# Rotating images by 180 degrees on one Trainium2 core: the first 2 KB of the last 32 rows loaded, brought in by three small transfers

## The chip, the cores and the metric

The kernel runs on one core of one Trainium2 chip. The metric is the device time of one execution in microseconds (us); less is better. The time of an execution is a little longer than its span, which runs from the first to the last instruction of the program in the profile.

## The reference

```python
x = np.random.randn(32, 3, 256, 256).astype(np.float32)

def reference(x):
    return np.rot90(x, k=2, axes=(-2, -1)).astype(np.float32)
```

Each of the 96 images of 256 x 256 float32 numbers is turned by 180 degrees. Seen as one row of 65,536 numbers, an image is simply reversed. Nothing is computed: 25.17 MB are read from HBM, put into reverse order within each image, and 25.17 MB are written.

## The kernel before

**Tiling.** An image is cut into four quarters of E = 16,384 numbers (64 KB). A tile has 128 partitions of E numbers, so it holds 32 images, one quarter in each partition; the whole input is three such tiles, `A`, `Bt` and `Ct`, which all stay in SBUF beside a scratch tile `T`. What follows calls one partition's 64 KB a row. Partition 4n + s holds quarter s of image n.

**Reversal.** It has two halves. VectorE (DVE) reverses every row in place: `swap` copies a piece from the row's end, read backwards, to `T`; then the mirror piece from the row's beginning, backwards, to the end; then `T` to the beginning. `turn` does this for a whole tile, in 4 pieces of 2048 columns for `A` and `Ct` (12 copies), and in 6 pieces of up to 1366 columns for `Bt` (18 copies). The store transfers do the rest: they write the four quarters of an image in reverse order (`o4[g][:, ::-1, lo:hi]`).

**Order of the transfers.** All transfers are issued by SP (SyncE) on one DMA queue, which feeds 16 DMA engines. The loads are issued at the very beginning, without any wait: `A` (line 56), `Bt` (line 56), then `Ct` in three parts (line 72): the 64 even rows, the 32 rows 1, 5, 9, ..., called `ahead`, and the 32 rows 3, 7, 11, .... In the trace's packet records each row is one packet, and between the small packets that tell of a transfer's end each DMA engine has 8 rows of `A`, 8 of `Bt`, then 4, 2 and 2 rows of `Ct`; then 8 rows of each of the three stores.

**When the first store is issued.** Tile dependencies would let the store of `A` go once `A` is turned. Two dependencies written by hand hold it back:

```python
*_, last_but_one, last = turn(Bt, 6)
after(last_but_one, ahead,
      "this copy starts when all loads but two rows are in")
first = store(A, 0, 0, E)
after(first, last, "the first store goes two copies after that")
```

The last but one copy of `Bt`'s turn waits until `ahead` has landed; after it comes the last copy, and then SP issues the stores of `A` and `Bt` (line 59). The turn of `Ct` waits for all three parts of `Ct`, and the store of `Ct` comes after that.

Of the kernel before, what the change touches and what calls it, by code (L numbers as in the profile page):

```python
# [2 lines left out]

os.environ.setdefault("NEURON_RT_ULTRASERVER_MODE", "4")

# [4 lines left out]


@with_exitstack
def kernel(
    ctx: ExitStack,
    tc: tile.TileContext,
    x: bass.AP,
    out: bass.AP,
):
    nc = tc.nc  # L20
    P = 128

    B, C, H, W = x.shape
    L = H * W
    G = 32
    E = L // 4
    J = E // 8

    x4 = x.rearrange("b c h w -> (b c) (h w)").rearrange(
        "(g n) (s e) -> g (n s) e", n=G, s=4)  # L30
    o4 = out.rearrange("b c h w -> (b c) (h w)").rearrange(
        "(g n) (s e) -> g n s e", n=G, s=4)

    pool = ctx.enter_context(tc.tile_pool(name="slots", bufs=1))
    A = pool.tile([P, E], x.dtype, tag="A")
    Bt = pool.tile([P, E], x.dtype, tag="B")
    Ct = pool.tile([P, E], x.dtype, tag="C")
    T = pool.tile([P, J], x.dtype, tag="T")

    def back(t, lo, hi):  # L40
        return t[:, hi - 1:(lo - 1 if lo else None):-1]

    def copy(dst, src):
        c = nc.vector.tensor_copy(out=dst, in_=src)  # L44
        tc.keep_in_program_order(c)
        return c

    def after(later, earlier, why):
        tc.add_manual_dep(
            later.ins, earlier.ins.name,  # L50
            mybir.DependencyInfo(
                mybir.DependencyClass.Sync, mybir.DependencyReason.DATA),
            reason=why)

    def load(t, g, lo, hi):
        return nc.sync.dma_start(out=t[:, lo:hi], in_=x4[g][:, lo:hi])  # L56

    def store(t, g, lo, hi):
        return nc.sync.dma_start(
            out=o4[g][:, ::-1, lo:hi], in_=t[:, lo:hi])  # L60

    def swap(t, lo, w):
        hi = E - lo - w
        return [
            copy(T[:, 0:w], back(t, hi, hi + w)),
            copy(t[:, hi:hi + w], back(t, lo, lo + w)),
            copy(t[:, lo:lo + w], T[:, 0:w])]

    half = E // 2

    def rows(first, step):
        return nc.sync.dma_start(
            out=Ct[first::step, :], in_=x4[2][first::step, :])

    load(A, 0, 0, E)
    load(Bt, 1, 0, E)
    rows(0, 2)
    ahead = rows(1, 4)
    rows(3, 4)

    def turn(t, pieces):
        done = []
        step = -(-half // pieces)
        for lo in range(0, half, step):
            done += swap(t, lo, min(step, half - lo))
        return done

    turn(A, 4)
# [5 lines that stand above are left out]
    store(Bt, 1, 0, E)  # L94
    turn(Ct, 4)
    store(Ct, 2, 0, E)


# [1 line left out]
_INS = ['x']  # L100
_OUTS = [((32, 3, 256, 256), 'float32')]


# [23 lines left out]
```

## Time and profile before

| | before |
|---|---|
| median of 3 runs | 122.09 us (121.94 to 122.11) |
| the profiled execution: time, span | 122.06 us, 120.3 us |
| DMA queue: share of 16 engines, mean rate | 97.3%, 418 GB/s |
| DVE busy | 45.2 us (38%), 42 copies |
| landing of `A` after its issue | 22.0 us |
| landing of the store of `Ct` after its issue | 42.7 us |

The profile counts the packets of the DMA engines, the copies on DVE and the issuing instructions of SP. A wait is put down to what ended it. In a view of the DMA, a packet's bytes are counted in the slice in which the packet starts, so that a high rate in a short slice says that several rows start there, and the number of rows can be read from it: a row of 64 KB in a slice of 0.2 us shows as 328 GB/s.

### The profile page before, as it was taken

The page shows a single profiled execution, that of the slowest core. Times are in us where ns is not written, and L with a number is a line of the kernel's source. Part 1 is how long each engine was busy: PE and PEld are TensorE (multiplying, and loading weights), DVE is VectorE, ACT ScalarE, POOL GpSimd, SP SyncE. Part 2 cuts the span into 40 slices and gives each one's busy share as a digit, 9 for nine tenths or more (in the row PEclk, how much of TensorE's full clock was granted, in tenths as well). Part 3 has the DMA queues.
Part 4 walks back from the last instruction along what each step waited for, and adds up shares of the span by engine and source line. Part 5 has one row for each costly group of instructions (what it writes and reads, how often), then busy time and mean ns, then how long its engine had stood idle before and what let it go on. Part 6 is the DMA issues. An engine that isn't in the chain of part 4 may idle for free.

```text
span 120.3 us, 101 instructions
## 1 busy us (share of the span) xinstructions
DVE 45.2 (38%) x42; POOL 0.2 (0%) x4
## 2 busy tenths in 40 slices
DVE  0000000499995099999459999400000000000000
POOL 0000000000000000000000000000000000000000
DMA  9889998899889988998899889988998889888980
GB/s 349 349 349 392 588 414 349 371 610 414 349 349 610 436 349 349 567 479 349 349 501 545 349 349 414 632 349 349 392 654 349 349 349 697 349 349 349 676 371 0
DMA packets 897, 50.33 MB, mean 418 GB/s; under 512 B 129, under 2 KB 129, under 8 KB 129
## 3 DMA queue, kind: packets, MB, share of 16 engines
q1 hardware_dynamic: 896, 50.33, 97.3%
q14 instruction: 1, 0.00, 0.0%
HBM read 25.17 MB, written 25.17 MB: 418 GB/s over the span
## 4 chain that ended last, share of the span: by engine, by line
DMA 34%; DVE 26%; another core or an unknown queue 2%; issue 1%; SPq 0%; DVEq 0%
DMA Bt<-in_x_dram 34%; DVE Bt L44 9%; DVE T L44 9%; DVE Ct L44 8%; SPq L56 0%; DVEq L44 0%
## 5 line engine op out<-in xcount | busy, mean ns | idle before, releaser
L44 DVE COPY T<-A 128x2048 f32<-128x2048 f32 x4 | 4.9, 1227 | 22.9 <-DMA A<-in_x_dram 22.8
L44 DVE COPY T<-Bt 128x1366 f32<-128x1366 f32 (+1 forms) x6 | 5.2, 874 | 4.5 <-DMA Bt<-in_x_dram 4.3
L44 DVE COPY T<-Ct 128x2048 f32<-128x2048 f32 x4 | 4.9, 1227 | 3.2 <-DMA Ct<-in_x_dram 3.1
L44 DVE COPY Bt<-T 128x1366 f32<-128x1366 f32 (+1 forms) x6 | 5.2, 872 | 0.2
L44 DVE COPY Bt<-Bt 128x1366 f32<-128x1366 f32 (+1 forms) x6 | 5.2, 872 | 0.2
L44 DVE COPY Ct<-T 128x2048 f32<-128x2048 f32 x4 | 4.9, 1227 | 0.1
L44 DVE COPY A<-A 128x2048 f32<-128x2048 f32 x4 | 4.9, 1227 | 0.1
L44 DVE COPY A<-T 128x2048 f32<-128x2048 f32 x4 | 4.9, 1227 | 0.1
L44 DVE COPY Ct<-Ct 128x2048 f32<-128x2048 f32 x4 | 4.9, 1227 | 0.1
L111 POOL MEMSET const-bfloat16-1.0<- 128x1 bf16 x1 | 0.1, 101 | 0.0
L111 POOL MEMSET const-uint8-127<- 128x1 uint8 x1 | 0.1, 101 | 0.0
L111 POOL MEMSET const-float32-0.0<- 128x1 f32 x1 | 0.1, 98 | 0.2 <-issue 0.2
L111 POOL MEMSET const-float32-1.0<- 128x1 f32 x1 | 0.1, 98 | 0.0
## 6 DMA issues: line engine op xcount, KB each, us to landing
Ct<-in_x_dram SPq DMA_DIRECT2D x3, 54.4
A<-in_x_dram SPq DMA_DIRECT2D x1, 22.0
Bt<-in_x_dram SPq DMA_DIRECT2D x1, 40.9
out_dram<-A SPq DMA_DIRECT2D x1, 22.3
out_dram<-Bt SPq DMA_DIRECT2D x1, 40.9
out_dram<-Ct SPq DMA_DIRECT2D x1, 42.7
```

The source lines that it names most:

```text
L44: c = nc.vector.tensor_copy(out=dst, in_=src)
L111: nc = _bacc.Bacc("TRN2", target_bir_lowering=False, num_devices=1)
```

## The change

The last of the loads, rows 3, 7, 11, ..., 127 of `Ct`, loses its first W = 512 columns (2 KB of each row). These 32 pieces are brought by three transfers of their own, of 15, 10 and 7 rows, which are issued after the even rows and before `ahead`. `ahead` itself, the copies and the stores stay as they are.

```diff
-    def rows(first, step):
+    def rows(first, step, end=P, lo=0, hi=E):
         return nc.sync.dma_start(
-            out=Ct[first::step, :], in_=x4[2][first::step, :])
+            out=Ct[first:end:step, lo:hi], in_=x4[2][first:end:step, lo:hi])
 
     load(A, 0, 0, E)
     load(Bt, 1, 0, E)
     rows(0, 2)
+    first, W = 3, 512
+    for k in (15, 10, 7):
+        rows(first, 4, first + 4 * (k - 1) + 1, 0, W)
+        first += 4 * k
     ahead = rows(1, 4)
-    rows(3, 4)
+    rows(3, 4, lo=W)
```

In the built program SP has three more transfers (15x512, 10x512, 7x512), and the last load is 32x15872 in place of 32x16384. The copies on DVE are the same 42 in the same order. The first copy of `Ct`'s turn waits for the even rows and the last load, and the second one, which reads the beginnings of the rows, for the three small transfers.

## The prediction

> **What bounds the kernel now.** I read the page's slices and its DMA queue first, then the waits, then the order of time where loads hand over to stores, then the DMA in short stretches. The page:
>
> ```profile
> DMA  9889998899889988998899889988998889888980
> GB/s 349 349 349 392 588 414 349 371 610 414 349 349 610 436 349 349 567 479 349 349 501 545 349 349 414 632 349 349 392 654 349 349 349 697 349 349 349 676 371 0
> q1 hardware_dynamic: 896, 50.33, 97.3%
> ```
>
> The 16 DMA engines are busy from the first slice to the last; the uneven rates are only whole rows counted where they start. In the packet records a 64 KB row takes 2.42 us on its engine, load or store (27.1 GB/s), and each engine has 24 rows to load and 24 to store: 48 x 2.42 = 116.2 us of a span of 120.28. So time can come or go only at the edges: the start, the handover from loads to stores, and the differences between the engines. DVE waits for transfers:
>
> ```profile
> DVE T L44 <- DMA A<-in_x_dram: 22.8, 1, 22.8
> DVE T L44 <- DMA Bt<-in_x_dram: 4.3, 1, 4.3
> DVE T L44 <- DMA Ct<-in_x_dram: 3.1, 1, 3.1
> ```
>
> There is one wait for each tile; `last_but_one`, which waits for `ahead`, is not among them. The order of time at the handover:
>
> ```profile
> 55.82 0.87 DVE L44 COPY T<-Bt 128x1362 f32<-128x1362 f32 x1
> 56.73 0.87 DVE L44 COPY Bt<-Bt 128x1362 f32<-128x1362 f32 x1
> 57.63 0.87 DVE L44 COPY Bt<-T 128x1362 f32<-128x1362 f32 x1
> 58.53 0.62 SPq L59 DMA_DIRECT2D out_dram<-A  x1
> 59.19 0.60 SPq L59 DMA_DIRECT2D out_dram<-Bt  x1
> 61.59 1.23 DVE L44 COPY T<-Ct 128x2048 f32<-128x2048 f32 x1 [3.09 <-DMA Ct<-in_x_dram]
> ```
>
> The copy at 56.73 follows the one at 55.82 at the usual step of 0.91 us: `ahead` had just landed. In the semaphore records its last of 16 landings is at 56.63, a slack of 0.10 us. The store goes at 58.53. How far the engines are apart is seen in short stretches, first where `ahead` ends and the last rows begin:
>
> ```profile
> 55.40:55.60 0.20, 0.20 (x1) 0.00 (x0) 1.00 1.52 655
> 55.60:55.80 0.20, 0.19 (x1) 0.00 (x0) 1.00 3.79 1638
> 55.80:56.00 0.20, 0.18 (x1) 0.00 (x0) 1.00 3.79 1638
> 56.00:56.20 0.20, 0.20 (x1) 0.00 (x0) 1.00 2.28 983
> 56.20:56.40 0.20, 0.20 (x1) 0.00 (x0) 1.00 0.76 328
> ```
>
> The last column is GB/s; 328 in 0.2 us is one row. So 2, 5, 5, 3 and 1 engines begin their last two rows in these stretches: the first engine is some 0.76 us ahead of the last (packets at 55.46 to 56.23), and as all rows take the same time, this lag is as old as the first row. Then the stores, from 60.2 to 61.4 in slices of 0.03 us:
>
> ```profile
> DMA  0000000099009099000099900099900000000000
> GB/s 0 0 0 0 0 0 0 0 2185 2185 0 0 2185 0 4369 4369 0 0 0 0 2185 6554 4369 0 0 0 2185 2185 2185 0 0 0 0 0 0 0 0 0 0 0
> ```
>
> 2185 is one row that starts there. Thirteen engines start storing from 60.45 to 60.87, three at 61.00, 61.03 and 61.06. The packet records of the loads end at 60.32 to 61.06. Sorted against the starts, the last three, and four more, go over to the stores within 0.01 us: their own loads are the limit. The other nine stand idle for some 0.1 us each (0.91 us in sum): the store's issue is their limit, the latest at 60.87. From there an engine needs 57.95 to 58.16 us for its 24 rows of stores, and the last ends at 119.13 (it began at 61.03). The last landing is at 119.47, and 0.81 us of closing make the span.
>
> **The change, part by part.** Sums are made against the profiled execution, 122.06 us (span 120.28, and 1.78 around it); the median of the runs, 122.09, is 0.03 above.
>
> *Three more issues on SP.* The three part transfers of `Ct` took 0.577, 0.586 and 0.597 us to issue. Three more move the issue of `ahead` from 2.24 to about 4.1 us and of the last load from 2.87 to about 4.8. The engines come to `ahead` at 50.6 us, so 46 us of earlier rows hide it: nothing. Without that cover it would be 3 x 0.63 = 1.9 us.
>
> *Bytes.* They are the same in sum. A piece of 2 KB is 1/32 of a row: 2.42 / 32 = 0.076 us. Each engine's last two rows lose 2 x 0.076 = 0.15 us. The transfers of 128, 64 and 32 rows gave each engine the same number of whole rows; going by them, 15, 10 and 7 rows are one row on each of 15, 10 and 7 engines. If all three begin at the same engine, seven engines have 3 pieces, three have 2, five have 1, and one has none: net +0.08, 0, -0.08 and -0.15 us. If they were spread evenly the net is 0. No row of this trace shows which engines they are. [...]
>
> *The price of a piece beyond its bytes.* From below: at every border between two transfers the packet records show the little end packet (9 ns) and the next row 6 ns after its start, and that row takes the usual 2.418 us. From above: the very first rows, with nothing in front of them, took 2.86 to 3.65 us, so 0.44 to 1.23 us of start that nothing hid. The pieces stand in a full queue behind a 64 KB row, as the borders do, so I take 0.01 us and keep 0.44 for the range. [...]
>
> *The wait for `ahead`.* The pieces go ahead of it, so an engine with three reaches its end 3 x 0.086 = 0.26 us later, one with two 0.17, with one 0.09. The slack is 0.10. What counts is the latest engine, at 56.22 by its end packet and 56.63 by its landing. If it is among the seven with three pieces, `ahead` lands at 56.89 and `last_but_one` starts 0.16 us late; with two, 0.07; with one or none, on time. Behind that copy stand the last copy, SP's issue of both stores, and the nine engines that are idle at the handover.
>
> *The handover.* With 0.16 us the latest of those nine starts storing at 61.03 and ends at 61.03 + 58.16 = 119.19. The late engines that have three pieces end their loads 0.08 + 3 x 0.01 = 0.11 us later: 61.14 to 61.17, and 58.0 to 58.1 us of stores make 119.15 to 119.24. Against 119.13 that is 0.06 to 0.11 us more. The turn of `Ct` begins at most 0.2 us later; it ends at 76.70, and its store is not reached by an engine before 99, so that costs nothing.
>
> Forecast: 122.06 + 0.1, rounded with the median's 0.03 to **122.2 us**, which is no change within the 0.2% (0.24 us) that a measurement of this kernel can tell.
>
> **The rivals.**
>
> *Evened out (faster side).* The late engines are those with one piece or none. Then `ahead` lands on time, the three late ones gain 0.08 to 0.15 us, and the end is set by the nine that wait for the store: 60.87 + 58.16 = 119.03, a gain of 0.10 us: 122.0. More is to be had only if the stores' rows, now 2.415 to 2.423 us in the mean by engine, come into a better step too: 24 x 0.008 = 0.2 us, together -0.3: 121.8. For it: the lags that the pieces could level are there (0.76 us). Against: the store's issue doesn't move, and it caps the gain.
>
> *The pieces are dear (slower).* Three short transfers in a row leave an engine's pipeline dry between them. It pays twice: at `ahead` and at the end of the loads. The store is late by 3 x (0.076 + p) - 0.10, and the end is 119.03 plus that. It decides by the 0.24 us from p = 0.07 us on. With p = 0.1 the store is 0.43 us late: +0.33, 122.4; with p = 0.2 it is 0.73: +0.63, 122.7; with 0.44 it is 1.45: +1.35, 123.4. For it: first rows have a start of 0.44 us and more, and a slack of 0.10 us has no room. Against: the borders at 6 ns, though each has a whole row behind it. It needs the late engine to be one with three pieces.
>
> *The split does not do what it says.* Evenly spread pieces cost 2 x 0.086 us ahead of `ahead`, 0.07 us beyond the slack, and nothing at the end of the loads: 122.1. On the other side, all pieces of a transfer on one engine: 32 x 0.076 = 2.4 us on it, 124.3.
>
> **How the numbers follow.** Forecast 0.34. Evened out 0.24, of which 0.18 with a better step, beyond 0.2%. Dear pieces 0.32. Evenly spread 0.06, on one engine 0.04. Faster 0.18; same 0.34 + 0.06 + 0.06 = 0.46; slower 0.32 + 0.04 = 0.36. The range goes from the evened-out case with the better step, 121.8, to dear pieces at p = 0.17, 122.6; dearer ones, and pieces on one engine, are left out, some 0.15 together.
>
> **What would show it.** Right: the copy after 55.8 us starts some 0.16 us after its turn, the store of `A` is issued near 58.7, the store rows start in a bunch that ends near 61.2, and the packet records show 2 KB packets of about 0.08 us. Wrong: 2 KB packets or gaps of 0.15 us and more, with the store issued after 58.9; or a store issued at 58.53 as before with starts that end before 61.0, which would be the evened-out case. A row time other than 2.42 us anywhere would break the whole sum.

## The result, and the profile after

| | before | after |
|---|---|---|
| median | 121.97 us (22 runs, 121.74 to 122.20) | 122.19 us (22 runs, 122.07 to 122.61) |
| ratio | | 1.0021, 95% interval 1.0014 to 1.0028 |
| profiled execution: time, span | 122.06, 120.3 us | 122.61, 120.8 us |

The change costs 0.2%, just at the bound of what the prediction called no change. The profiled execution of the changed kernel is the slowest of its 22; the experiment `again` below gives a second profile, at the median, and sizes are read from both.

The page of the changed kernel (slices, DMA queue, and the one group of copies whose idle time is new):

```profile
DMA  9889998999889988997799889988998899889980
q1 hardware_dynamic: 960, 50.33, 97.0%
L44 DVE COPY Bt<-Bt 128x1366 f32<-128x1366 f32 (+1 forms) x6 | 5.2, 872 | 0.4 <-DMA Ct<-in_x_dram 0.2
```

The queue is as full as before (97.0% of the 16 engines' span, before 97.3%). There are 64 packets more: 32 pieces of 2 KB and their 32 end packets. The last line is `last_but_one`: now it waits for a load of `Ct`. The order of time at the handover, changed kernel:

```profile
56.08 0.87 DVE L44 COPY T<-Bt 128x1362 f32<-128x1362 f32 x1
57.19 0.87 DVE L44 COPY Bt<-Bt 128x1362 f32<-128x1362 f32 x1 [0.24 <-DMA Ct<-in_x_dram]
58.09 0.87 DVE L44 COPY Bt<-T 128x1362 f32<-128x1362 f32 x1
58.99 0.64 SPq L59 DMA_DIRECT2D out_dram<-A  x1
59.67 0.60 SPq L59 DMA_DIRECT2D out_dram<-Bt  x1
61.90 1.23 DVE L44 COPY T<-Ct 128x2048 f32<-128x2048 f32 x1 [2.94 <-DMA Ct<-in_x_dram]
```

From 56.08 to 57.19 is 1.11 us where the step was 0.91: the wait costs the store 0.20 us. The rest of the shift of 58.53 to 58.99 is this execution's own: Bt landed at 42.37 instead of 42.11, because one engine's first row ended only at 5.78 us. Against Bt's landing the store is issued after 16.62 us, before it was 16.42. The starts of the stores' rows, 60.2 to 61.4 us in slices of 0.03 us, changed kernel:

```profile
DMA  0000000000000009900909099009099909000000
GB/s 0 0 0 0 0 0 0 0 0 0 0 0 0 0 0 2185 2185 0 0 2185 0 4369 0 2185 4369 0 0 4369 0 4369 2185 2185 0 2185 0 0 0 0 0 0
```

Fifteen engines start from 60.66 to 61.21; the sixteenth, the late one, starts at 61.40, past the window. And one wait at the very end has moved. SP's waits in the kernel before:

```profile
SPq L122 <- DMA out_dram<-Ct: 19.3, 1, 19.3
SPq L122 <- DMA out_dram<-Bt: 19.3, 1, 19.3
SPq L122 <- DMA out_dram<-A: 3.5, 1, 3.5
```

and in the changed kernel:

```profile
SPq L126 <- DMA out_dram<-Ct: 42.3, 1, 42.3
```

Before, SP closes the program by waiting for the three stores one after the other, and the wait for the store of `Ct` is the last. Now it waits for the store of `Ct` first, and the instructions that wait for the other transfers still have to be run after the last landing. What that is worth is found below.

### The profile page after: what moved, and what is told of

Its sections match the earlier page's. It is cut to its first block, busy times and chain, and to the rows that moved or that the text cites. A ratio compares the mean times of both kernels' runs of the same rounds, so it can differ in the third digit from the quotient of the medians.

```text
span 120.8 us, 107 instructions
## 1 busy us (share of the span) xinstructions
DVE 45.2 (37%) x42; POOL 0.2 (0%) x4
## 4 chain that ended last, share of the span: by engine, by line
DMA 34%; DVE 25%; another core or an unknown queue 2%; issue 1%; SPq 0%; DVEq 0%
DMA Bt<-in_x_dram 34%; DVE Bt L44 9%; DVE T L44 8%; DVE Ct L44 8%; SPq L56 0%; DVEq L44 0%
## 6 DMA issues: line engine op xcount, KB each, us to landing
Ct<-in_x_dram SPq DMA_DIRECT2D x2, 51.4
```

## The experiments

The kernels share the runs of the kernel before that were made on their chip. Three times are read from the semaphore and instruction records of each profile: the store's issue after Bt's last landing, what the copy `last_but_one` waits (0.03 to 0.04 us is the usual gap), and the closing, from the last landing to the end of the span.

| kernel | ratio to before (95%) | store after Bt's landing | gap before last_but_one | closing |
|---|---|---|---|---|
| before | 1 | 16.42 us | 0.03 us | 0.81 us |
| after | 1.0021 (1.0014 to 1.0028) | 16.62 | 0.24 | 0.92 |
| again | 1.0015 (1.0007 to 1.0024) | 16.68 | 0.30 | 0.92 |
| pieces_late | 1.0023 (1.0015 to 1.0032) | 16.64 | 0.26 | 0.92 |
| no_hold | 1.0005 (0.9995 to 1.0016) | 16.41 | 0.04 | 0.92 |
| pieces_late_no_hold | 1.0014 (1.0006 to 1.0023) | 16.42 | 0.03 | 0.92 |
| before_no_hold | 0.9999 (0.9991 to 1.0008) | 16.42 | 0.03 | 0.82 |
| even_pieces | 1.0005 (0.9996 to 1.0013) | 16.57 | 0.19 | 0.79 |
| delay_small | 1.0012 (1.0003 to 1.0020) | 16.63 | 0.04 | 0.81 |
| delay_large | 1.0015 (1.0007 to 1.0024) | 16.82 | 0.04 | 0.82 |
| store_early | 1.0020 (1.0009 to 1.0031) | 15.51 | 0.04 | 0.81 |
| pieces_store_early | 1.0034 (1.0022 to 1.0047) | 15.51 | 0.03 | 0.92 |
| store_slightly_early | 0.9993 (0.9985 to 1.0002) | 16.25 | no hold | 0.81 |
| eleven_transfers | 1.0883 (1.0863 to 1.0903) | after 10 us of wait | 10.05 | 0.92 |

### again: the changed kernel a second time

> The changed kernel once more, for a second profile, since the first one was of an execution 0.4 us above the median. Theory (late store): `ahead` lands some 0.2 us later against the landing of Bt than before (14.52 us between the two landings before), the copy behind it starts 0.2 us late, the store of A is issued 16.6 us after Bt's landing instead of 16.42, and the time is 0.2 to 0.3 us over the kernel before. Rival (dear pieces): the 2 KB packets or the gaps beside them take 0.15 us and more each. Rival (phases): the store is issued as before, and the rows of the stores take longer in the mean than 2.415 to 2.423 us.

Measured: 122.19 us, ratio 1.0015; its profiled execution took 122.19 too. The same two steps, in order of time:

```profile
55.64 0.87 DVE L44 COPY T<-Bt 128x1362 f32<-128x1362 f32 x1
56.81 0.87 DVE L44 COPY Bt<-Bt 128x1362 f32<-128x1362 f32 x1 [0.30 <-DMA Ct<-in_x_dram]
58.61 0.64 SPq L59 DMA_DIRECT2D out_dram<-A  x1
```

`ahead` lands 14.79 us after Bt, before it was 14.52: 0.27 us later. The 32 pieces took 0.084 us each in the packet records, and from one end packet to the next it is 0.086. So the pieces are not dear in the queue, and the wait is there. The stores' rows took 2.423 us in the mean, before 2.424: the third theory (phases) finds nothing here.

### pieces_late: the pieces behind `ahead`

```diff
+    ahead = rows(1, 4)
     for k in (15, 10, 7):
         rows(first, 4, first + 4 * (k - 1) + 1, 0, W)
         first += 4 * k
-    ahead = rows(1, 4)
```

> The three small transfers are issued after `ahead` and before the last load, all else as in the changed kernel. Late store: `ahead` lands as before the change, no wait at last_but_one, the store is issued 16.42 us after Bt's landing, and the time is that of the kernel before within 0.1 us, or up to 0.1 us below it. Dear pieces or phases: the same pieces, the same shift between the engines at the end of the loads, so the loss of 0.2 us stays.

Measured: 1.0023, all of the loss stays. By the late-store theory the loss should have gone, but the store did not go on time either: the copy waited 0.26 us though no piece stood ahead of `ahead`. `ahead` landed 14.74 us after Bt, 0.22 later than before. In this profile some rows of the loads ran long (2.43 us in the mean, before 2.42), and besides, the landing was told later: on the latest engine the end packet was at 56.38 and the landing at 56.87, 0.50 us, where Bt's lag was 0.32. So this kernel did not do what it was built for, and `pieces_late_no_hold` was needed.

### no_hold: the copy does not wait for `ahead`

```diff
-    after(last_but_one, ahead,
-          "this copy starts when all loads but two rows are in")
```

> The changed kernel without the dependency of last_but_one on `ahead`; the first store still goes after the last copy of Bt. Late store: the store is issued 16.42 us after Bt's landing, and the time is that of the kernel before within 0.1 us. Dear pieces or phases: 0.2 us over the kernel before, as the changed kernel is.

Measured: 122.06 us against 121.99, 1.0005: most of the loss is gone (`again`, on the same chip, has 122.19). The pieces lie just as unevenly here, so their unevenness alone does not cost 0.2 us. The order of time of this kernel has the usual step and the store where it was:

```profile
55.80 0.87 DVE L44 COPY T<-Bt 128x1362 f32<-128x1362 f32 x1
56.71 0.87 DVE L44 COPY Bt<-Bt 128x1362 f32<-128x1362 f32 x1
58.51 0.63 SPq L59 DMA_DIRECT2D out_dram<-A  x1
```

### before_no_hold: the control, the same edit on the kernel before

> The kernel before without the dependency of last_but_one on `ahead`. By its trace the copy hardly waited (0.00 to 0.01 us), so the store goes at the same time: the same time as before within 0.05 us. This is the control for the changed kernel without the hold (0.07 us over the kernel before): if the hold itself is worth something, this control is over by as much.

Measured: 0.9999 (0.9991 to 1.0008). The hold itself costs and brings nothing that is seen in the kernel before.

### pieces_late_no_hold: both edits

> The three small transfers after `ahead`, and no dependency of last_but_one on `ahead`. With the dependency this order cost 0.23 us, and its trace had a wait of 0.23 us in front of last_but_one although no piece stood ahead of `ahead`. Late store: without the wait the store is issued 16.42 us after Bt's landing, and the loss falls to what the changed kernel without the hold has, 0.05 to 0.1 us. Rival (the pieces at the end of the loads cost the time, whatever the store does): 0.2 us stays.

Measured: 1.0014, so +0.17 us where 0.05 to 0.1 was expected; with the wait it was 1.0023. The difference is about 0.1 us, as between `again` and `no_hold`, but the two intervals here overlap, so this pair alone does not show it; the rest of the loss stays without the wait. Together with `no_hold` the loss without a wait is 0.06 and 0.17 us, some 0.1 us that the late store does not explain. The closing in the table has the size for it, and it is the end of the span itself: it is 0.92 us in every kernel with the three small transfers, and 0.79 to 0.82 in every kernel with 8 or 9 transfers, a difference of 0.11 us.

### eleven_transfers: three transfers more, without any pieces

```diff
-    rows(0, 2)
+    for first in (0, 2, 4, 6):
+        rows(first, 8)
```

> The kernel before with its 64 even rows of Ct in four transfers of 16 rows (rows 0, 8, ...; 2, 10, ...; and so on), one row on each engine: no pieces, the same bytes in the same place, but 11 transfers in place of 8, as many as the changed kernel has. Theory (closing): in every trace with the three small transfers there are 0.92 us between the last landing and the end of the span, in the kernels with 8 or 9 transfers 0.79 to 0.82, because SP's closing waits go through the eight semaphores of the transfers in a fixed order of pairs, and with 11 transfers the last store has a semaphore of the second pair, with two more waits behind it. So the closing is 0.92 us here too, and the time some 0.11 us over the kernel before, plus 3 borders of 6 ns. Rival (small transfers of 15, 10 and 7 rows cost the 0.1 us that is left without the wait): closing 0.81 us and the time of the kernel before.

Measured: the closing is 0.92 us as expected, and the time is 1.0883, which neither theory had. The waits of DVE and of SP in this kernel:

```profile
DVE Bt L44 <- DMA Ct<-in_x_dram: 10.1, 1, 10.1
```

```profile
SPq L123 <- DMA out_dram<-Ct: 42.1, 1, 42.1
```

The second line is the single closing wait of the changed kernel again, with no small transfer in the program. In the instruction records SP waits for the eight semaphores of its transfers in a fixed order, in four instructions. With 8 transfers the last store has a semaphore of the last pair, with 9 too (`even_pieces`), with 11 of the second pair: after its landing come two instructions more, one every 0.064 us. The time of this kernel says nothing of 0.1 us, though, since the rows of its four transfers of 16 took 4.8 to 5.1 us each, in the mean of a transfer, instead of 2.42 (see the end). So the longer closing is read from the traces; no run has it as its only difference in time.

### delay_small and delay_large: what a late store costs in the kernel before

```diff
+    last = copy(T[:, 0:8], Bt[:, 0:8])      # delay_large: 0:400
     first = store(A, 0, 0, E)
```

> The kernel before with one small extra copy (128x8) between the last copy of Bt and the first store, no small transfers. By the trace (0.872 us for 1366 columns, 1.227 for 2048) the copy costs about 0.16 us and 0.03 to the next, so the store is issued some 0.2 us later. Late store: of the 0.2 us about half to all shows in the time, +0.1 to +0.2 us, as much as the change costs. Rivals: a store 0.2 us later is hidden behind the engines' own loads, 0.

> The kernel before with one extra copy of 128x400 between the last copy of Bt and the first store: some 0.4 us of delay, where the copy of 8 columns put the store 0.21 us later against Bt's landing and cost 0.12%. Late store: beyond what the engines' own loads hide, each 0.1 us of delay costs 0.1 us, so +0.2 over the small delay: +0.3 to +0.35 us. If the small delay's cost was only chance: 0 to 0.1 us.

Measured: the store is 0.21 and 0.40 us late against Bt's landing, at +0.15 us (1.0012) and +0.18 us (1.0015). The first is as expected; the second is only half of what was expected, so this late store does not cost its full lateness. The two times alone do not differ clearly (their intervals overlap). The starts of the stores' rows in `delay_large`, same window as above:

```profile
DMA  0000000000909990090009990000999000000000
GB/s 0 0 0 0 0 0 0 0 0 0 2185 0 2185 8738 2185 0 0 4369 0 0 0 2185 2185 4369 0 0 0 0 2185 2185 2185 0 0 0 0 0 0 0 0 0
```

The store is issued at 58.91 us, 0.39 later than in the kernel before, but the rows start at 60.50 to 61.11 instead of 60.45 to 61.06, and between loads and stores the engines stand idle for 0.96 us in sum instead of 0.91. In these two profiles a row so does not start at a fixed time after the issue, and idle engines at the handover do not account for the cost; how a late store lengthens the time stays open. By the times alone, a store that is 0.2 to 0.26 us late, as after the change, is worth an estimated 0.1 to 0.2 us.

### even_pieces: two pieces on every engine

```diff
-    for k in (15, 10, 7):
-        rows(first, 4, first + 4 * (k - 1) + 1, 0, W)
-        first += 4 * k
+    rows(first, 4, P, 0, W)
```

> The changed kernel with the same 32 pieces in one transfer of 32 rows ahead of `ahead`, two pieces on each engine, so nothing is levelled. Late store: the last engine reaches the end of `ahead` 0.17 us later and, as in the other kernels with pieces, the landing is told some 0.1 us later after its end packet; the store is 0.2 to 0.3 us late, and the time 0.2 to 0.3 us over the kernel before. Rival (the unevenness of 3, 2, 1 and 0 pieces costs the time, not the wait): back to the kernel before, within 0.1 us.

Measured: 1.0005, 122.00 against 121.96 us. The expected loss of 0.2 to 0.3 us is not there: the store was 0.16 us late, the landing of `ahead` came 0.36 us after its end packet, no later than in the kernel before, and with 9 transfers the closing is short. Scaled from the two delays, 0.16 us of lateness are worth an estimated 0.07 to 0.11 us, which the interval holds. The time is also what the rival foretold, so this run does not exclude that the unevenness costs something; `no_hold`, with the same uneven pieces as the changed kernel, is 0.06 us over the kernel before, the longer closing included. What the records show is that the three small transfers of 15, 10 and 7 rows bring what one of 32 rows does not, or less of it: a wait of 0.20 to 0.26 us instead of 0.16, and a closing of 0.92 us instead of 0.79.

### store_early and pieces_store_early: the store one copy earlier

```diff
-    after(first, last, "the first store goes two copies after that")
+    after(first, last_but_one, "the first store goes two copies after that")
```

(`pieces_store_early` has the pieces, and no hold.)

> The kernel before, with the first store one copy (0.91 us) earlier: after last_but_one instead of after the last copy. Late store: the nine engines that stand idle for 0.1 us at the handover find their stores in the queue, only the late engines' own loads set the end: 0 to 0.1 us less than before. Rival (something else than idle engines is what a store's time of issue changes, and 0.91 us early is as bad as late): 0.1 us and more over the kernel before.

> The changed kernel without the dependency of last_but_one on `ahead`, and with the first store after last_but_one: the pieces level the engines a little, and no engine waits for a store. Late store: no loss from the wait; the end is set by the latest engine's own loads, which in most traces here have 0 to 2 pieces: 0.05 to 0.15 us below the kernel before. If the pieces cost something by themselves (the kernel without the hold was 0.06 us over): the same as before, or slightly over.

Measured: 1.0020 and 1.0034, slower by 0.24 and 0.41 us, where the late-store theory had both faster. The rival was right: the store 0.91 us early costs 0.24 us, where the one 0.40 us late costs 0.18. In the second kernel the longer closing of 0.92 us comes on top. The starts of the stores' rows in `store_early`, same window as above:

```profile
DMA  0000000000000009999909990990909000000900
GB/s 0 0 0 0 0 0 0 0 0 0 0 0 0 0 0 4369 2185 2185 2185 2185 0 4369 2185 4369 0 2185 2185 0 2185 0 2185 0 0 0 0 0 0 2185 0 0
```

The first row starts at 60.67 us, in the kernel before at 60.45, although the store was issued 1 us earlier. No engine is idle now; the loads themselves end later. In the packet records the last row of the loads took 2.56 to 3.04 us on fourteen engines and 2.44 on two, instead of 2.42 to 2.44. Why these rows took longer was not found.

### store_slightly_early: 0.17 us earlier

```diff
-    *_, last_but_one, last = turn(Bt, 6)
-    after(last_but_one, ahead,
-          "this copy starts when all loads but two rows are in")
+    *_, last_but_one, last = turn(Bt, 5)
+    last = copy(T[:, 0:450], Bt[:, 0:450])
```

> The kernel before with the store some 0.13 us earlier: Bt turned in 5 pieces of 1639 columns in place of 6, an extra copy of 128x450 after them, no dependency on `ahead`. Late store in a narrow sense (idle engines alone): 0.03 to 0.1 us less. If a store that is queued behind running loads lengthens their last rows already here, as it did at 0.91 us: the same as before or up to 0.1 us more.

Measured: 121.94 against 121.98 us, 0.9993 with an interval to 1.0002: some 0.04 to 0.09 us less, with nothing at all inside the interval. In its records ten engines' last load row already takes 2.46 to 2.65 us, and the idle time at the handover is down to 0.1 us in sum. No kernel here beats the kernel before clearly.

## Why the prediction was right, point by point

The forecast of 122.2 us, some 0.1 above before, met a median of 122.19 and a difference of 0.2 us. The wait that it named is there, but its terms were not all of the right size, one was missing, and the way from the late store to the end of the time was another than it thought. The absolute figure is partly luck: the forecast stood on 122.06 and 122.09 us, from three runs, where the median of 22 runs is 121.97, so a base that was 0.1 us too high made up for a change that was 0.1 us too small. One of its signs, the store at 58.99, lies past the 58.9 that it gave, together with dear pieces, as a sign of being wrong; but 0.26 of the shift of 0.46 us was that execution's late landing of Bt, and the pieces were not dear.

- **Price of a piece: right.** Forecast 0.086 us with its end, measured 0.086 from one end packet to the next; by the rows' rate (2.42 / 32) 0.076 of it are bytes. The rival of dear pieces is out; a single piece in each of two profiles took 0.26 and 0.29 us.
- **How the pieces are spread: right.** Linked by their ends and starts, the packets of five of six traces fall into seven engines with 3 pieces, three with 2, five with 1 and one with none (the sixth links two packets ambiguously). The semaphore records agree: each of the three transfers has one update some 0.4 us after its issue (in `after` at 3.61, 4.46 and 5.22 us), long before its rows are moved, and 15, 10 and 7 landings from 51.4 us on. The records do not number the engines, so which of them a transfer takes is not shown.
- **Slack of 0.10 us: wrong, it was about zero.** `ahead` landed at 56.63 and the copy started at 56.73, but 0.10 us is what a copy with a wait instruction in front of it took after a landing: Bt landed at 42.11 and its first copy started at 42.21 (`A`'s first copy, which has no such instruction, started 0.02 us after its landing). The copy had not waited, and had nothing to spare.
- **Lateness of `ahead`: 0.20 to 0.27 us, where 0.26 less the slack made 0.16.** The bytes on the latest engine were fewer than feared in one profile (one piece), three pieces in `again`. But a term was missing: behind the small transfers a landing follows its end packet after 0.42 to 0.49 us in the mean of `ahead`'s engines in the kernels with the three small transfers ahead, where the kernels without pieces have 0.34 to 0.38.
- **Price of the late store: 0.06 to 0.11 forecast; about 0.1 to 0.2 measured, and not in the way forecast.** The size goes by the difference of the kernels with and without the hold (1.0018 as the mean of `after` and `again`, less 1.0005, is 0.16 us; 1.0023 less 1.0014 is 0.11, with overlapping intervals) and by the delays. The prediction had nine engines stand idle until the store reaches them, and start as much later as the store is late. `delay_large` contradicts that: 0.39 us later in the issue, some 0.05 us later in the starts, and no more idle time to speak of. What the late store changes instead is not known.
- **The closing: missing, 0.11 us.** The prediction took the 0.81 us after the last landing as fixed. It counted three more issues on SP at nothing, which is right, but not what three more transfers do to the order of SP's closing waits. Late store (0.11 to 0.16 us) and closing (0.11) make 0.22 to 0.27 us, and 0.18 to 0.26 were measured. So the forecast of +0.1 is half of what was measured, with one term too few and the wait's two terms too small.
- **Evened out: half right.** Its premise holds: relative to the mean, the first row ends 0.23 us late on the engines with no piece, 0.11 late with one, 0.06 to 0.09 early with two or three (six traces). The pieces do go to the engines that are ahead. But the end did not get earlier: the store's issue moved the wrong way, and `no_hold`, where it stays in place, is not faster than the kernel before either. That the levelling alone would bring anything was not shown.

## What to carry to other kernels

A step that hangs on a landing has slack only beyond the time that a landing takes to start it, here 0.10 us with a wait instruction in front of the copy; compare with a wait that is plainly there. The added transfers of 15, 10 and 7 rows had two prices here that no byte shows: the copy that waits for `ahead` got its landing 0.20 to 0.27 us later, and SP's closing waits ended in another order, with a closing of 0.92 us instead of 0.81. Where a store is timed against the end of the loads, measure both sides before moving it: here 0.2 us late cost 0.15 us, and 0.9 us early cost 0.24.

## What the runs showed of the hardware

- **Landings beside the transfers of 15, 10 and 7 rows.** The even rows' last landing comes 9.67 us after Bt's in `before` and `delay_small`, and 9.86 to 9.90 in the four profiles where the pieces follow it; in `pieces_late` and `pieces_late_no_hold` it is `ahead` that is late, 14.74 and 14.70 us instead of 14.52. With one transfer of 32 small rows the even rows have 9.68. So in these six profiles the landing of the transfer just in front of those of 15, 10 and 7 rows comes 0.2 us later. Why was not tested.
- **Issue.** The transfers of 15, 10 and 7 rows took SP 0.98, 0.76 and 0.71 us to issue, the other loads 0.37 to 0.63. `ahead` was so issued at 4.83 us, where the prediction had 4.1; it was hidden here all the same.
- **Sixteen rows eight partitions apart ran at half rate.** In `eleven_transfers` such rows took 4.8 to 5.1 us in the mean of a transfer instead of 2.42; 16 rows in that time are 205 to 219 GB/s, where 2.42 us would make 433. Why was not tested.
- **Rows of stores are not all alike.** Their mean was 2.424 us in `before`, and 2.418 to 2.419 us in both kernels with the early store, in `store_slightly_early` and in the profile of `before_no_hold`, in which the engines stood idle at the handover for 0.04 to 0.3 us in sum instead of 0.91: 24 rows make 0.12 to 0.14 us. Idle time alone does not decide it: `no_hold` has 0.3 us too and rows of 2.421 us. The gain is smaller than what the early stores lost at the handover.
